# Gate projections of the stick-breaking heads moved into a filler queue, with an earlier start of the fillers

## The chip, the cores and the metric

The kernel runs on one core of a Trainium2 chip. The metric is the device time of one execution in microseconds (us), lower is better. A core has a matrix engine (TensorE, called PE in the profile, with its weight loads as PEld), VectorE (DVE), ScalarE (ACT), GpSimd (POOL) and a queue engine for transfers (SyncE, SP). Transfers are started from the queues of SP, ACT and POOL.

## The reference

Two layers of a decoder trunk, on 1024 rows of width 1024 in f32. Each layer normalises its input with a modulation computed from a conditioning vector, makes one wide projection of it, runs two attentions in parallel and merges them:

```python
mod = jax.nn.silu(c) @ ada_w + ada_b
shift, scale, gate = jnp.split(mod, 3, axis=-1)
h = rms_norm(x, norm_g) * (1 + scale[:, None]) + shift[:, None]
proj = h @ w_in
(sb_q, sb_k, sb_v, sb_z, n_q, k_c, v_c, k_s, v_s, k_w, v_w, n_z, n_g, m_a, m_b) = jnp.split(...)
a = stick_breaking_attention(heads(sb_q, 8), heads(sb_k, 8), heads(sb_v, 8))
a = a.reshape(B, S, 512) * jax.nn.silu(sb_z)
...
b = native_sparse_attention(q, kc, vc, ks, vs, kw, vw, n_g)   # softmax, 8 heads
b = b * jax.nn.silu(n_z)
y = jax.nn.sigmoid(m_a) * (a @ w_proj_a) + jax.nn.sigmoid(m_b) * (b @ w_proj_b)
return x + gate[:, None] * (y @ w_out)
```

Stick-breaking attention uses sigmoids of the scores and a running product in place of a softmax. `sb_z` is the gate projection that the change moves; `n_z` is the sparse heads' gate. Each is 512 columns wide.

## The kernel before

A projection is computed in f32 precision from three products of split operands (high x high, high x low, low x high), so a unit of 128 x 512 outputs takes 24 matmuls (`mm3_gen`, L188 to L199). A group is 256 columns of the weights: four units of 128 columns by 512 rows, or eight units of 128 rows by 256 columns for values. Units are accumulated in the PSUM tile "proj", which has two buffers, and then evicted by ScalarE and VectorE. Weights are loaded from SP, split by ScalarE and VectorE, and loaded one group ahead in the order of a list (`plan_layer`, `take`).

A layer has these stages.

1. `early` (L703): keys and values of the sparse heads, the compressed keys and values, a loop of eight value units (`n_unit`, L808 to L811), the query groups, and then four groups of gate projections (L819 to L838): first the two of the sparse heads, then the two of the stick-breaking heads. A gate unit is evicted by a Sigmoid on ScalarE (L830) and a product on VectorE (L831) and stored in DRAM (`SZ`). Beside the gate units run the modulation steps: one loads 512 KB of `ada_w` (tile "ada", two buffers) from SP, and VectorE adds it, scaled, to an accumulator (L362, L364). Layer 0 has 24 steps (its own gate and the next layer's scale and shift), layer 1 has 8. Two are written behind each unit, from the first gate unit on. `issue_after` keeps a step's VectorE instruction behind that unit's product; the load on SP is free of it. When all groups are done, `gate_rows` and `cols` turn the accumulators into rows and columns with small matmuls on PE (L411, L373).
2. `nsa`: sparse attention, as a list of jobs: 8 compressed-score jobs and 32 head jobs (2 groups x 4 query blocks m x 4 heads). Its scores go through Exp on ScalarE (L1006, L1097, L1099).
3. `sb`: stick-breaking attention, 8 heads x 4 query blocks m. Its scores go through Sigmoid (L1245, L1246), VectorE's scan (L1249) and product (L1250).
4. `output`: merging and the output projection.

Beside stages 2 and 3 run the fillers: generators of projection matmuls in the queue `fill`. `queue_projections` puts in two query, two key and two value groups of the stick-breaking heads (kind "sb") and then eight groups of the merging gates (kind "gate", evicted by a plain copy, L1271). `run_jobs` writes the bursts of a job's value products together with the scores of the next job, and after each burst calls `pump`, which writes filler matmuls for a share of the job's planned time. The planned costs are 0.213 us for a 512-column matmul and 0.107 us for a 256-column one; the planned times of the jobs are `nsa_us` and `sb_us` by m, `cmp_us` for a compressed-score job, and `start_us` for the first scores of a stage. `drain_fill("sb")` between the stages writes what is left of the "sb" groups, `drain_fill()` after stage 3 all that is left.

What is written last is not always what runs last: the framework orders the instructions of each engine again, by the written order as priority and by its own estimate of when inputs are ready. Every engine then works through its order strictly, each instruction waiting for its inputs. The build puts an ACT_TABLE_LOAD on ScalarE ahead of an activation whose function is not in the table loaded last.

## Time and profile before

| what | us |
|---|---|
| median of 3 runs | 2232.81 |
| lowest and highest run | 2227.79, 2235.55 |
| the profiled execution | 2227.61 |
| its span, first to last instruction | 2225.8 |
| PE busy in the span | 2124.4 |
| VectorE busy | 1573.0 |
| ScalarE busy | 1129.9 |

The profile is one execution. Its times count from the span's start. Matmuls overlap, so PE's busy time holds the tail of each; what counts for PE is how far apart the starts are. In layer 0 the early stage ends at about 291, sparse attention at about 690, stick-breaking attention at about 954; in layer 1 at about 1374, 1778 and 2040. A wait is put down to the instruction that came last by the profile.

### The profile page before, as it was taken

What the parts mean: (1) busy time and instruction counts of PE and PEld (TensorE: products, weight loads), DVE (VectorE), ACT (ScalarE), POOL (GpSimd) and SP (SyncE); (2) the same over time, 40 slices, a digit from 0 to 9 for tenths busy, and PEclk for the clock granted to TensorE, in tenths of its full rate; (3) what the DMA queues carried; (4) which work ended last, traced back from release to release, by engine and by line L of the source; (5) the groups of instructions that cost most, each with busy time, mean ns of one, the idle gap of its engine ahead of it and who ended that gap; (6) DMA issues with size and microseconds to landing.
All of it is one profiled execution on the core that took longest, in us unless ns stands there. A gap on an engine that the chain in (4) does not pass through costs nothing.

```text
span 2225.8 us, 36846 instructions
## 1 busy us (share of the span) xinstructions
PE 2124.4 (95%) x13128; PEld 1833.5 (82%) x13128; DVE 1573.0 (71%) x3722; ACT 1129.9 (51%) x2489; POOL 73.0 (3%) x242
## 2 busy tenths in 40 slices
PE   4999999999999999999999998999999999999999
PEld 3898778988887777779889986889898877777899
DVE  5768558868765877886766852887788487787643
ACT  4433147656565655663433421665666465656410
POOL 2200000000000000010011000000000000001000
PEclk8999999999999999999999999999999999999999
DMA  7545852253116445275555355222522364534443
GB/s 287 113 136 189 251 154 81 91 152 94 64 48 159 128 130 129 81 245 177 164 151 161 107 192 141 90 90 82 146 92 68 97 151 113 146 98 166 148 124 104
DMA packets 254104, 297.05 MB, mean 133 GB/s; under 512 B 38888, under 2 KB 201568, under 8 KB 253920
## 3 DMA queue, kind: packets, MB, share of 16 engines
q1 hardware_dynamic: 213152, 250.65, 37.4%
q10 hardware_dynamic: 36224, 29.37, 5.1%
q0 software_dynamic: 4544, 14.68, 2.3%
q8 instruction: 103, 1.69, 0.3%
q14 instruction: 81, 0.66, 0.1%
HBM read 206.28 MB, written 83.89 MB: 130 GB/s over the span
## 4 chain that ended last, share of the span: by engine, by line
PE 66%; DVE 18%; DMA 7%; issue 4%; ACT 3%; POOL 1%; SPq 0%; ACTq 0%; DVEq 0%; POOLq 0%
PE proj L194 15%; PE proj L198 15%; PE proj L196 15%; PE tr L885 5%; DVE C L1249 4%; PE av L905 4%; PE av L904 3%; PE sc L872 3%; PE sc L873 3%; DVE wl L137 3%; DMA ada<-in_ada_w 2%; DVE E L1250 2%; DVE w L137 2%; DMA q<-QK 1%; DMA actlo<-AD 1%
## 5 line engine op out<-in xcount | busy, mean ns | idle before, releaser
L194 PE MATMUL proj<-acthi,w 128*128 128x512 f32 x1312 | 537.6, 410 | 3.0 <-ACT acthi L136 2.2
L196 PE MATMUL proj<-actlo,w 128*128 128x512 f32 x1312 | 538.0, 410 | 0.0
L198 PE MATMUL proj<-acthi,w 128*128 128x512 f32 x1312 | 537.2, 409 | 0.0
L136 ACT CAST w<-raw 128x512 fp32r<-128x512 f32 (+1 forms) x296 | 183.3, 623 | 227.3 <-PE proj L198 129.7
L194 PEld LDWEIGHTS proj<-acthi,w 128*128 128x128 f32 x1312 | 250.2, 191 | 43.6 <-ACT acthi L136 2.7
L137 DVE TENSOR_TENSOR wl<-tr,wh 128x512 fp32r<-128x512 f32 (+2 forms) x432 | 257.0, 611 | 40.7 <-ACT wh L136 38.3
L196 PEld LDWEIGHTS proj<-actlo,w 128*128 128x128 f32 x1312 | 250.0, 191 | 38.1 <-DVE actlo L137 0.8
L198 PEld LDWEIGHTS proj<-acthi,w 128*128 128x128 f32 x1312 | 249.6, 190 | 37.1 <-DVE w L137 0.2
L137 DVE TENSOR_TENSOR w<-raw,w 128x512 fp32r<-128x512 f32 (+1 forms) x296 | 202.5, 689 | 81.9 <-ACT w L136 80.6
L136 ACT CAST wh<-tr 128x512 fp32r<-128x512 f32 (+2 forms) x432 | 221.3, 527 | 76.4 <-PE tr L885 71.3
L194 PE MATMUL proj<-w,acthi 128*128 128x256 f32 (+1 forms) x768 | 221.5, 289 | 5.4 <-DVE s L137 2.4
L905 PE MATMUL av<-wl,V 128*128 128x256 f32 (+1 forms) x864 | 217.6, 285 | 7.6 <-DVE wl L137 7.4
L198 PE MATMUL proj<-w,actlo 128*128 128x256 f32 (+1 forms) x768 | 221.1, 288 | 0.0
L196 PE MATMUL proj<-w,acthi 128*128 128x256 f32 (+1 forms) x768 | 220.0, 286 | 0.0
L904 PE MATMUL av<-wh,V 128*128 128x256 f32 (+1 forms) x864 | 216.7, 271 | 1.2 <-DVE o L923 0.5
L1249 DVE TENSOR_TENSOR_SCAN C<-C 128x128 f32<-128x128 f32 (+7 forms) x128 | 172.7, 1350 | 55.0 <-ACT C L1245 54.5
L885 PE MATMUL tr<-ident,E 128*128 128x128 f32 x1152 | 187.4, 276 | 24.2 <-DVE E L1250 23.4
L885 PEld LDWEIGHTS tr<-ident,E 128*128 128x128 f32 x1152 | 139.1, 140 | 68.1 <-DVE E L1250 35.4
L905 PEld LDWEIGHTS av<-wl,V 128*128 128x128 f32 x864 | 162.7, 188 | 31.0 <-DVE wl L137 19.7
L872 PE MATMUL sc<-kk,q 128*128 128x512 f32 (+3 forms) x512 | 176.8, 346 | 8.8 <-DVE mx L1085 4.1
L873 PE MATMUL sc<-kk,q 128*128 128x512 f32 (+3 forms) x512 | 175.5, 343 | 0.0
L904 PEld LDWEIGHTS av<-wh,V 128*128 128x128 f32 x864 | 163.0, 189 | 13.7 <-ACT wh L136 3.6
(247 smaller groups left out, 3902.8 us busy)
## 6 DMA issues: line engine op xcount, KB each, us to landing
raw<-in_w_in SPq DMA_DIRECT2D x168, 256.0 KB, 3.0
ada<-in_ada_w SPq DMA_DIRECT2D x48, 512.0 KB, 5.1
kk<-QK SPq DMA_DIRECT2D x48, 512.0 KB, 8.6
q<-QK ACTq DMA_DIRECT2D x64, 256.0 KB, 4.2
QK<-s SPq DMA_DIRECT2D x32, 512.0 KB, 3.0
MD<-sz SPq DMA_DIRECT2D x64, 256.0 KB, 2.5
QK<-s SPq DMA_DIRECT2D x48, 256.0 KB, 3.9
VD<-s SPq DMA_DIRECT2D x48, 256.0 KB, 2.0
```

What stands on the lines that cost most here:

```text
L136: nc.scalar.copy(hi, src)
L137: nc.vector.tensor_tensor(lo, src, hi.bitcast(F32), ALU.subtract)
L194: nc.tensor.matmul(ps, lh, rh, start=(x == 0), stop=False)
L196: nc.tensor.matmul(ps, lh, rl, start=False, stop=False)
L198: nc.tensor.matmul(ps, ll, rh, start=False, stop=(x == n - 1))
L872: nc.tensor.matmul(ps, q, k[:, 0, c0:c1], start=True, stop=False)
L873: nc.tensor.matmul(ps, q, k[:, 1, c0:c1], start=False, stop=not masks)
L885: nc.tensor.transpose(pt[:, x * P:x * P + P], b, self.ident)
L904: nc.tensor.matmul(ps[:, c:d], lhsT, hi[:, a:b], start=(first and x == 0), stop=False, skip_group_check=True)
L905: nc.tensor.matmul(ps[:, c:d], lhsT, lo[:, a:b], start=False, stop=(last and x == n - 1), skip_group_check=True)
L1249: nc.vector.tensor_tensor_scan(rev, rev, rev, 1.0, ALU.mult, ALU.bypass)
L1250: nc.vector.tensor_tensor(e[:, 0:nk], e[:, 0:nk], c[:, 1:nk + 1], ALU.mult)
```

## The change

Four things are changed.

- The two gate groups of the stick-breaking heads leave `early`. They become fillers of kind "sb" at the head of the queue, evicted by a new helper `silu_gate` with the same Sigmoid, product and store as before.
- The modulation steps are written earlier: one behind each of the eight value units, then two behind each of the eight gate units that stay. The tile "ada" has four buffers.
- `run_jobs` first writes fillers for a planned time `start`, ahead of the first scores: 12.0 us for the sparse part, 1.5 us for the stick-breaking part. Another 1.5 us are spread over the first scores, where it was 3.0.
- The planned times of the stick-breaking jobs grow from 1.34, 2.87, 4.77, 6.04 to 1.55, 3.35, 5.4, 6.8 us.

```diff
-        self.sb_us = (1.34, 2.87, 4.77, 6.04)
+        self.sb_us = (1.55, 3.35, 5.4, 6.8)
         self.cmp_us = 1.48
-        self.start_us = 3.0
+        self.start_us = 12.0
...
-    def run_jobs(self, jobs):
+    def run_jobs(self, jobs, start):
+        self.pump(start)
         for n in range(len(jobs) + 1):
...
-            us = jobs[n - 1][2] if n else self.start_us
+            us = jobs[n - 1][2] if n else 1.5
...
-            a = self.tl(pool, [P, D], F32, "ada", bufs=2)
+            a = self.tl(pool, [P, D], F32, "ada", bufs=4)
...
             w = self.take()
+            steps = []
+            self.gate, gate_rows = self.mod_gate(l, pool, steps)
+            if l + 1 < self.depth:
+                cols = self.mod_ab(l + 1, pool, steps)
+
+            def mod_steps(n, ins):
+                with tc.issue_after(ins.ins):
+                    for f in steps[:n]:
+                        f()
+                del steps[:n]
+
             for t in range(NT):
                 ps = self.n_unit(w, t, act, 280)
-                self.store_v(ps, t, 8)
+                ins = self.store_v(ps, t, 8)
                 nc.scalar.activation(self.G[:, t, :], ps[:, 256:280], AF.Sigmoid)
+                mod_steps(1, ins)
...
-            for z in range(4):
+            for z in range(2):
                 w = self.take()
-                if z == 0:
-                    steps = []
-                    self.gate, gate_rows = self.mod_gate(l, pool, steps)
-                    if l + 1 < self.depth:
-                        cols = self.mod_ab(l + 1, pool, steps)
                 for u in range(2):
                     for half in range(2):
-                        ps = self.t_unit(w, u, half, act)
-                        s = self.tl(self.stage, [P, 512], F32, "sz")
-                        nc.scalar.activation(s, ps, AF.Sigmoid)
-                        ins = nc.vector.tensor_tensor(s, ps, s, ALU.mult)
-                        with tc.issue_after(ins.ins):
-                            for f in steps[:2]:
-                                f()
-                        del steps[:2]
-                        r0 = z * 256 + u * 128
-                        nc.sync.dma_start(self.SZ[r0:r0 + P, half * 512:half * 512 + 512], s)
+                        mod_steps(2, self.silu_gate(self.t_unit(w, u, half, act), z * 256 + u * P, half))
...
+    def silu_gate(self, ps, r0, half):
+        nc = self.nc
+        s = self.tl(self.stage, [P, 512], F32, "sz")
+        nc.scalar.activation(s, ps, AF.Sigmoid)
+        ins = nc.vector.tensor_tensor(s, ps, s, ALU.mult)
+        nc.sync.dma_start(self.SZ[r0:r0 + P, half * 512:half * 512 + 512], s)
+        return ins
...
-            self.run_jobs(jobs)                     # nsa
+            self.run_jobs(jobs, self.start_us)
...
-            self.run_jobs(jobs)                     # sb
+            self.run_jobs(jobs, 1.5)
...
-                    if what == "qk":
+                    if what == "z":
+                        self.silu_gate(ps, r0 + u * P, half)
+                    elif what == "qk":
...
+        for z in range(2):
+            self.fill.append(("sb", t_group("z", 512 + z * 256)))
         for a in range(2):
             self.fill += [("sb", t_group("qk", 512 + a * 256)), ("sb", t_group("qk", a * 256)), ("sb", v_group(a * 4))]
```

`split` and `store_v` now return their VectorE instruction, so that `issue_after` can name it.

## Rows read from the trace of the kernel before

**Rows 1.** Page, part 1: busy us, share of the span, instructions.

```profile
PE 2124.4 (95%) x13128; PEld 1833.5 (82%) x13128; DVE 1573.0 (71%) x3722; ACT 1129.9 (51%) x2489; POOL 73.0 (3%) x242
```

**Rows 2.** PE in order of time, layer 1's first scores: start, us, what.

```profile
1373.60 0.67 PE L194 MATMUL proj<-acthi,w 128*128 128x512 f32 x1
...
1380.84 0.39 PE L194 MATMUL proj<-acthi,w 128*128 128x512 f32 x1
...
1382.24 0.40 PE L194 MATMUL proj<-acthi,w 128*128 128x512 f32 x1
1389.16 1.86 PE L996 MATMUL sc<-KCS,q 128*128 128x16 f32 x8 [6.52 <-DMA q<-QK]
...
1393.14 0.63 PE L198 MATMUL proj<-acthi,w 128*128 128x512 f32 x1
1393.57 0.63 PE L194 MATMUL proj<-acthi,w 128*128 128x512 f32 x1
```

**Rows 3.** Busy us (instructions) per stretch: PE, PEld, DVE, ACT, POOL, PEclk, DMA, GB/s.

```profile
100.00:130.00 30.00, 26.66 (x201) 25.30 (x200) 14.83 (x50) 9.20 (x25) 0.00 (x0) 1.00 0.66 201
194.00:239.00 45.00, 45.00 (x200) 36.43 (x200) 30.41 (x54) 10.80 (x20) 0.00 (x0) 1.00 0.80 250
310.00:370.00 60.00, 59.10 (x368) 49.56 (x368) 54.20 (x206) 45.96 (x130) 0.32 (x2) 1.00 0.27 84
700.00:730.00 30.00, 26.60 (x159) 20.22 (x158) 27.87 (x38) 21.84 (x50) 0.89 (x9) 1.00 0.51 133
730.00:950.00 220.00, 207.63 (x1185) 167.41 (x1183) 175.92 (x234) 134.10 (x297) 9.21 (x57) 1.00 0.43 120
1388.00:1392.00 4.00, 2.84 (x12) 2.68 (x12) 0.76 (x4) 0.23 (x1) 0.00 (x0) 0.50 1.03 204
1810.00:2035.00 225.00, 211.96 (x1211) 170.80 (x1209) 180.18 (x241) 137.48 (x304) 7.13 (x54) 1.00 0.44 120
```

**Rows 4.** 730 to 950: PE's waits (us, times, longest), then the chain's shares.

```profile
PE tr L885 <- DVE E L1250: 9.3, 15, 1.0
PE av L905 <- DVE wl L137: 3.0, 8, 0.7
...
by line: DVE C L1249 17.7%; DVE E L1250 10.0%; PE proj L196 9.7%; PE proj L198 9.5%; PE proj L194 9.3%; PE tr L885 8.4%; DVE wl L137 5.3%; PE av L905 5.1%; issue 5.0%; PE av L904 4.0%; PE sc L873 2.5%; PE sc L872 2.4%; DVE w L137 2.0%; ACT 
```

**Rows 5.** PE in order of time, layer 0's first sparse scores.

```profile
303.81 1.04 PE L996 MATMUL sc<-KCS,q 128*128 128x16 f32 x8 [0.17 <-DMA q<-QK]
```

**Rows 6.** PE in order of time, end of layer 1's stick-breaking part.

```profile
2021.65 0.55 PE L885 MATMUL tr<-ident,E 128*128 128x128 f32 x3 [0.91 <-DVE E L1250]
...
2031.50 0.55 PE L885 MATMUL tr<-ident,E 128*128 128x128 f32 x3 [0.84 <-DVE E L1250]
...
2051.29 0.79 PE L194 MATMUL proj<-acthi,w 128*128 128x512 f32 x1 [2.23 <-ACT acthi L136]
```

**Rows 7.** ACT in order of time, layer 1: ACTq issues transfers.

```profile
1372.69 8.19 ACTq L942 DMA_DIRECT2D q<-QK  x4
```

**Rows 8.** 194 to 285 by line: busy us, mean ns, idle us before.

```profile
L364 DVE SCALAR_TENSOR_TENSOR acc<-ada,silu_c,acc 128x1024 f32<-128x1024 f32 x21 | 27.0, 1284 | 20.3 <-DMA ada<-in_ada_w 20.3
...
L830 ACT ACTIVATE sz<-proj 128x512 f32<-128x512 f32 x15 | 9.0, 599 | 43.5 <-PE proj L198 39.6 <-DVE sz L831 3.9
```

**Rows 9.** ACT in order of time, the first instructions.

```profile
0.74 1.28 ACT L514 ACT_TABLE_LOAD   x1 [0.74 <-PEq L1452]
2.03 0.20 ACT L514 ACTIVATE warm<-ones 128x1 f32<-128x1 f32 x1
```

**Rows 10.** Lines L1006 and L1245: table loads, ns, first and last start.

```profile
L1006 ACT ACT_TABLE_LOAD  x2: 1283/1283/1283, 297.6 to 1380.9; - x2
...
L1245 ACT ACT_TABLE_LOAD  x2: 1283/1283/1283, 692.7 to 1778.7; - x2
```

**Rows 11.** Page, part 6: transfers, count, KB each, us to landing.

```profile
ada<-in_ada_w SPq DMA_DIRECT2D x48, 512.0 KB, 5.1
```

More of the change, by code (lines that the diff above doesn't have):

```diff
@@ L136, in split @@
         nc.scalar.copy(hi, src)
-        nc.vector.tensor_tensor(lo, src, hi.bitcast(F32), ALU.subtract)
+        return nc.vector.tensor_tensor(lo, src, hi.bitcast(F32), ALU.subtract)
     def rsqrt(self, pool, ss, n, inv, tag, on_pool=False):
@@ L848, in store_v @@
         src = ps[:, 0:256].rearrange("p (h d) -> p h d", d=HD)
-        self.split(src, vt[:, :, 0:64], vt[:, :, 64:128])
+        ins = self.split(src, vt[:, :, 0:64], vt[:, :, 64:128])
         nc.sync.dma_start(self.VD[t * P:(t + 1) * P, h0:h0 + 4, :], vt.bitcast(F32))
+        return ins
     def load_stack_k(self, pool, row, tag="kk"):
```

## The prediction

> **What bounds the kernel now.** I read the page's busy times first [rows 1]: the matmul engine (PE) is busy for 95% of the span, VectorE for 71%, ScalarE for 51%. A busy PE is not PE at its peak: in a dense stretch two neighbouring 512-column projections begin 0.23 us apart while each is shown as 0.39 us long [rows 2]. So a gap shown as idle hides about 0.16 us more. The change keeps the number of matmuls; it can win nothing but waits, and lose nothing but new ones.
>
> The table by stretches [rows 3] says where waits are. The first half of the gate projections in layer 0 (194 to 239) has none: PE is busy for 45.00 of 45 us, ScalarE for 10.80. In the first jobs of sparse attention (310 to 370) PE is busy for 59.10 of 60, but VectorE for 54.20 and ScalarE for 45.96: three engines are close to full. In stick-breaking attention PE is idle for 3.4 of the first 30 us (700 to 730), then for 12.4 of 220 and, in layer 1, 13.0 of 225. Who ends those waits [rows 4]: VectorE's product after the scan (9.3 us, 15 waits) and its low parts (3.0 us, 8). The chain in that stretch lies on VectorE for 17.7 + 10.0 + 5.3 + 2.0 = 35%.
>
> Single waits remain. In layer 1 PE has nothing but fillers after 1373.60, begins the last at 1382.24 and then waits 6.52 us until the queries of the first sparse job land at 1389.16 [rows 2]; the granted clock behind that idle time is 0.50, the lower level (1.2 of 2.4 GHz), and matmuls start 0.43 us apart for a while [rows 2, 3]. In layer 0 the same place costs 0.17 us [rows 5]: there the fillers ahead of the scores lasted long enough. At the end of layer 1's stick-breaking part PE waits 0.91 and 0.84 us in the last job, then 2.23 us for an activation half [rows 6].
>
> **The change, part by part.** The planner counts 0.213 us per 512-column matmul, 20.45 us per group of 4 units, 20.54 us per value group. The profile's spacing is 0.233 us (the seven starts from 1380.84 to 1382.24 give 1.40 / 6), so a planned us is 1.09 us of PE. Before, a layer queues 122.9 us of "sb" and 163.6 us of "gate" filler, 286.5; the sparse part asks for 3.0 + 8 x 1.48 + 8 x 19.03 = 167.1, so 119.4 is left for the stick-breaking part, which asks for 3.0 + 8 x 15.02 = 123.2: the queue runs dry about 3.8 planned us before its end. After, two gate groups (8 units, 40.9 planned, 8 x 24 x 0.233 = 44.7 us of PE) join: 327.4. The sparse part asks for 12.0 + 1.5 + 164.1 = 177.6, stick-breaking for 1.5 + 1.5 + 8 x 17.1 = 139.8, and 10.0 is left to drain. So the 44.7 us that leave the dense early stage come back in three places: 11.5 us before the first sparse scores, 22.3 us spread over the stick-breaking jobs, 10.9 us at the end. Each is worth the waits that it covers.
>
> *Front of the sparse part.* 56 matmuls (13.1 us) now stand ahead of the first scores. In layer 1 it is 15.6 us from 1373.6 to 1389.2, of which 9.0 were covered; the new cover leaves about 2.5 us. That is worth 4.0 us of wait and the slow matmuls (about 13 at 0.43 instead of 0.23, 2.6 us): 6.5 us, bounds 2 and 9.3. The lower bound is there since ScalarE spends 8.19 us on issuing the query loads [rows 7] and evicts nothing meanwhile; with two PSUM buffers the third unit can be held up. Layer 0: 0, bounds -2 and +2.
>
> *Stick-breaking jobs.* 22.3 us more filler a layer against 12.4 + 23 x 0.16 = 16 us of waits and some 5 in the first 30 us, 21 in all. What falls into time that VectorE paces is free; by the chain that is 35%, 7.8 us a layer, 15.6 in all. Bounds: 0 (the fillers land where PE sets the pace) and 21 a layer.
>
> *End.* A queue that isn't dry covers the last job's waits, 0.91 + 0.84 a layer and their hidden parts (layer 0 repeats the pattern), and in layer 1 the 2.23 us: 6 us in all, bounds 2 and 8.
>
> *Activation tables.* This is the price. A gate unit ends in a Sigmoid (599 ns, [rows 8]); the sparse jobs run on Exp. The trace has 5 table loads: one at the start, one at the first Exp and one at the first stick-breaking Sigmoid of each layer, each 1283 ns [rows 9, 10]. So the two functions don't share a table. Of a layer's 8 queued Sigmoids two finish inside the 12 us ahead of the scores, before any Exp; the other six come one by one, 5.1 planned us apart, among jobs of 1.97 and 4.16 planned us with four Exps each. Each costs a load to Sigmoid and one back: 12 loads, 15.4 us of ScalarE a layer, in the stretch of 60 us that holds 45.96 us of it already: 61.4 of 60. Queued behind them are the high parts of transposed tiles, for which VectorE's low parts and then PE's value products wait. But a load stands ahead of the instruction that needs it and can run while that one's input is awaited, and the 14.0 us of ScalarE's idle time there are such waits. I take half on the path, 7.7 us a layer, 15.4 in all; bounds 0 and 30.8.
>
> *Modulation loads.* 24 loads of 512 KB in layer 0 (8 in layer 1, [rows 11]) and as many accumulations of 1284 ns [rows 8] move from the first twelve of sixteen gate units to the eight value units and all eight gate units that stay. In 100 to 130 VectorE is busy for 14.83 of 30 us, so 8 x 1.28 = 10.3 us fit, but PE already loses 3.3 us there and DMA stands at 0.66 [rows 3]. In the gate stage 21 accumulations waited 20.3 us for their loads [rows 8] beside a PE that never stopped; four buffers send a pair of loads one unit earlier. Now the last pair is due with the last gate unit, and the columns of the next layer's modulation wait for it, where four units stood behind. On SP a load that waits for its buffer holds up value stores and the weights of the query groups. I take 2 us for the value units (both layers) and 2 us for the end of layer 0's early stage; bounds -1 and 10.
>
> *The rest.* A gate eviction uses VectorE for one product where a query or key eviction uses it for one subtraction; some 6 such units a layer take the place of plain copies in the sparse part: 1 us in all, bounds 0 and 4. The gate rows are read back in stick-breaking jobs only, long after.
>
> Sum: -6.5 - 15.6 - 6 + 15.4 + 4 + 1 = -7.7 us. On the profiled execution (2227.61, its span 2225.8) that is 2219.9. That execution lies 5.2 us under the median of the three; I carry the difference to the median: 2232.8 - 7.7 = **2225.1**.
>
> **The rivals.**
> 1. *The table loads hide* in ScalarE's waits, and the price drops from 15.4 to about 1: -22 us, 2211. For it: the idle time is nearly as large as the loads. Against: VectorE, which waits for ScalarE's high parts, is at 90% there.
> 2. *ScalarE becomes the bound of the first sparse jobs* (slower). It decides from the point where the loads exceed what idle ScalarE time can take, and 61.4 us in 60 is past it. Then all 30.8 us are on the path, and with half of the stick-breaking gain the sum is -6.5 - 7.8 - 6 + 30.8 + 5 = +15.5, 2248. For it: all five loads of the trace came on an idle engine, so what a load costs right behind other work isn't in the 1283 ns. Against: behind a load nothing comes; the warm-up's ends at 2.03 and the next activation begins at 2.03 [rows 9]. The Trainium skill (ScalarE: Activation LUTs, What ACT_TABLE_LOAD costs) counts a drain of about 1380 ns beside the 1283, 2.66 us a switch; by it, as an estimate, a layer's 12 switches would want 32 us of ScalarE, 18 us more than the stretch has idle, and the sum would be about +13 us. No load of this trace follows work closely enough to show that drain.
> 3. *The change doesn't do what it says.* The order on PE is not the program's (fillers ran ahead of the scores in both layers before, too), so the 12 us may replace only what was moved up anyway, and the extra fillers of the stick-breaking jobs may land on time that PE paces: gains and prices cancel, about 0, 2233.
>
> **How the numbers follow.** A measurement of this kernel can tell about 0.3%, 6.7 us, from no change. Forecast 0.42 (-20 to -2, a bit over half of it beyond 6.7), rival 1 0.22, rival 2 0.22, rival 3 0.14. Faster: 0.25 + 0.22 = 0.47; same: 0.17 + 0.14 = 0.31; slower 0.22. The range reaches from rival 1 with half of the stick-breaking gain's upper room (about -29, 2204) to rival 2 (2247). The forecast's own range is 2213 to 2231.
>
> **What would show it.** 29 table loads instead of 5, the 24 new ones between the first sparse scores and some 70 us later; idle PE there up by 8 us a layer if I am right, by 1 in rival 1, by 15 in rival 2. The wait before layer 1's first sparse scores under 2.5 us, with the clock at its upper level. Idle PE in each stick-breaking part down from 16 to 8 us. No wait of 2 us at layer 1's end. The gate stage shorter by 44.7 us in each layer. I would be wrong if the early stage shrank by clearly less than that, or if the queued gate units stood elsewhere than ahead of the first scores.

## The result, and the profile after

| what | before | after |
|---|---|---|
| median, us (after: 4 runs beside runs of before) | 2232.53 | 2245.51 |
| lowest to highest of after, us | | 2241.76 to 2246.65 |
| ratio of the medians, 95% interval | | 1.0059 [1.0040, 1.0078] |
| the profiled execution, us | 2227.61 | 2245.80 |
| its span, us | 2225.8 | 2244.0 |

The change costs 13 us. The two profiled executions lie 18.2 us apart, since that of before lies some 5 us under its median.

Page of after, part 1, which answers [rows 1], and the engine line of its part 4:

```profile
PE 2134.3 (95%) x13128; PEld 1840.7 (82%) x13128; DVE 1577.4 (70%) x3722; ACT 1160.6 (52%) x2513; POOL 72.3 (3%) x242
...
PE 66%; DVE 15%; DMA 7%; ACT 5%; issue 5%; POOL 1%; SPq 0%; ACTq 0%; DVEq 0%; POOLq 0%
```

PE runs the same 13128 matmuls. ScalarE has 24 instructions and 30.7 us more. No engine's total explains a loss of 18 us.

The busy times hide a part of PE's waits, so I made a tally of the trace: for each form of matmul the median spacing of two neighbouring starts in before; what the spacings have above it in sum counts as stall. All kernels here come to 2032 us of spacing without stall; the rest is in this table (us of stall per stage, profiled executions; the columns are explained with the experiments):

| stage | before | after | after again | e5 | e4 | e11 | e10 | e16 |
|---|---|---|---|---|---|---|---|---|
| early, layer 0 | 43.8 | 49.4 | 48.4 | 48.7 | 50.0 | 49.2 | 48.3 | 49.8 |
| to the first sparse scores | 5.1 | 7.3 | 5.6 | 5.1 | 5.7 | 7.2 | 5.7 | 4.1 |
| sparse, to the first stick-breaking scores | 22.5 | 30.1 | 29.5 | 24.2 | 26.0 | 24.4 | 21.5 | 21.5 |
| stick-breaking | 32.6 | 28.0 | 28.4 | 32.4 | 24.5 | 25.5 | 21.3 | 21.4 |
| output of layer 0, early of layer 1 | 9.6 | 23.2 | 24.5 | 15.8 | 20.5 | 17.1 | 16.4 | 12.0 |
| layer 1: to the first sparse scores | 8.2 | 2.4 | 3.0 | 7.7 | 8.6 | 1.5 | 2.9 | 3.8 |
| layer 1: sparse | 23.0 | 25.6 | 26.3 | 22.3 | 27.1 | 25.3 | 22.6 | 21.4 |
| layer 1: stick-breaking | 31.2 | 27.6 | 27.3 | 30.7 | 24.6 | 24.2 | 21.3 | 21.3 |
| layer 1: output | 4.1 | 4.3 | 4.2 | 3.5 | 4.1 | 2.6 | 2.0 | 2.4 |
| sum | 180.2 | 197.7 | 197.3 | 190.5 | 191.1 | 177.1 | 162.1 | 157.6 |

Each column is one execution, and single executions scatter. Up to 660 us after, after again (e9), e10 and e13 run the same instructions in the same order on every engine, and yet PE's matmul number 3901 starts 657.7, 655.0, 651.7 and 654.4 us behind its first. So a difference of some 3 us in one row, up to 6 in a sum of rows, can be chance; the medians below decide on the kernels.

The gain at layer 1's first sparse scores is there (5.2 to 5.8 us), and so is a part of that in the stick-breaking jobs (3.6 to 4.6 us a layer). New are 4.6 to 5.6 us in layer 0's early stage, some 7 us up to the first stick-breaking scores of layer 0 and 3 in layer 1, and 14 to 15 us between the end of layer 0's stick-breaking part and the end of layer 1's early stage.

**Front of the sparse part.** PE in after, layer 1 (start, us, what, idle before and its releaser), which answers [rows 2]; 6.52 us of wait have become 0.68:

```profile
1368.05 0.58 PE L1005 MATMUL sc<-KCS,q 128*128 128x16 f32 x4 [0.68 <-DMA q<-QK]
```

A window over it shows the granted clock at 1.00, the upper level (columns as in [rows 3]):

```profile
1366.00:1370.00 4.00, 3.32 (x19) 2.54 (x18) 1.58 (x6) 1.45 (x2) 0.00 (x0) 1.00 1.10 240
```

**Stick-breaking jobs.** Windows of the same lengths in after, without each part's first 30 us, which answer [rows 3]:

```profile
711.00:931.00 220.00, 211.50 (x1193) 171.59 (x1192) 169.91 (x227) 131.67 (x289) 5.01 (x51) 1.00 0.42 115
1798.00:2023.00 225.00, 216.17 (x1217) 175.22 (x1215) 171.13 (x229) 132.62 (x291) 5.01 (x51) 1.00 0.42 114
```

PE's idle time fell from 12.4 to 8.5 and from 13.0 to 8.8 us. But at the head of this part PE now waits for the queries (PE in after, the last filler and the first scores in layer 0, the first scores in layer 1):

```profile
671.09 0.40 PE L196 MATMUL proj<-actlo,w 128*128 128x512 f32 x1
676.19 0.45 PE L881 MATMUL sc<-kk,q 128*128 128x128 f32 x1 [4.70 <-DMA q<-QK]
...
1768.12 0.30 PE L881 MATMUL sc<-kk,q 128*128 128x128 f32 x1 [3.43 <-DMA q<-QK]
```

Before has one such wait, in layer 0, and none in layer 1:

```profile
694.73 0.30 PE L872 MATMUL sc<-kk,q 128*128 128x128 f32 x1 [2.26 <-DMA kk<-QK]
```

**Value units of layer 1.** ScalarE, VectorE, SP and PE of after, in four extracts:

```profile
1222.42 0.59 ACT L136 CAST s<-tr 128x512 fp32r<-128x512 f32 x1 [1.43 <-DMA VD<-s]
1228.74 0.37 ACT L136 CAST s<-proj 128x256 fp32r<-128x256 f32 x1 [5.72 <-DMA QK<-s]
1229.60 0.19 ACT L823 ACTIVATE G<-proj 128x24 f32<-128x24 f32 x1 [0.49 <-DVE s L137]
...
1229.14 0.42 DVE L137 TENSOR_TENSOR s<-proj,s 128x256 fp32r<-128x256 f32 x1 [5.41 <-ACT s L136]
...
1220.32 0.33 SPq L858 DMA_DIRECT2D VD<-s  x1
1221.52 0.33 SPq L361 DMA_DIRECT2D ada<-in_ada_w  x1
1222.12 3.94 SPq L776 DMA_DIRECT2D QK<-s  x4
...
1225.56 0.27 PE L198 MATMUL av<-xs,w 128*128 128x192 f32 x1
1229.84 0.40 PE L194 MATMUL proj<-w,acthi 128*128 128x280 f32 x1 [4.01 <-ACT G L823]
...
1231.20 0.44 PE L196 MATMUL proj<-w,acthi 128*128 128x280 f32 x1
1231.44 0.44 PE L198 MATMUL proj<-w,actlo 128*128 128x280 f32 x1
```

Read it from below. PE stands for 4 us, since both PSUM buffers wait for evictions. The eviction on ScalarE waits 5.72 us, not for PE but for a store out of the staging tile "s" (QK<-s): the tile has two buffers, and neither is free until its keys or values have left it. On SP a modulation load (L361, 512 KB) stands between those stores. Behind the wait matmuls of 280 columns start 0.23 us apart, not 0.13; the granted clock there is 0.56:

```profile
1230.00:1233.50 3.50, 3.50 (x17) 3.50 (x18) 2.29 (x3) 0.56 (x2) 0.00 (x0) 0.56 0.68 164
```

The accumulations themselves no longer wait for their loads (by line, which answers [rows 8]):

```profile
L365 DVE SCALAR_TENSOR_TENSOR acc<-ada,silu_c,acc 128x1024 f32<-128x1024 f32 x28 | 35.8, 1277 | 0.1
```

**End of layer 0's stick-breaking part.** POOL, ScalarE and PE of after:

```profile
958.96 2.06 POOL L1352 DMA_DIRECT2D actlo<-AD  x3 [13.83 <-PE proj L198]
964.54 2.05 POOL L1352 DMA_DIRECT2D actlo<-AD  x3 [3.52 <-PE proj L198]
...
965.58 1.14 ACT L136 CAST acthi<-actlo 128x512 fp32r<-128x512 f32 x2 [1.84 <-DMA actlo<-AD]
...
966.25 0.50 PE L194 MATMUL proj<-acthi,w 128*128 128x512 f32 x1 [1.78 <-ACT acthi L136]
```

The output stage loads the attention's result into the activation halves that the fillers read. POOL issues the loads into a half only when the last filler matmul on that half is done ("<-PE proj L198"). In after the last filler is evicted 15.0 us behind the last merge of attention, in before 3.0 us ahead of it; the loads start 7.4 to 14.4 us behind that merge, in before from 14.4 us ahead of it (POOL of before):

```profile
939.93 2.10 POOL L1339 DMA_DIRECT2D actlo<-AD  x3 [5.87 <-PE proj L196]
```

From the last job's last matmul on the strict mask (936.7) up to the first matmul on the merged tile (yh, 1014.9) there are 7.1 us of stall, in before 2.8. In layer 1 the wait that the remainder was to cover is still there (2.23 us in [rows 6]):

```profile
2057.59 0.50 PE L194 MATMUL proj<-acthi,w 128*128 128x512 f32 x1 [1.74 <-ACT acthi L136]
```

**The clock behind the waits.** In nine stretches of after, the one at 1230 among them, the granted clock is at its lower level; before has five. In a tally of the same kind 24.0 and 16.9 us of the stall lie inside these stretches, so some 7 of the 17 us between the two come with the lower clock (after again has 22.2 us there, e11 15.5, e10 13.9, e16 9.0). Three that before has no match for, behind a wait for sparse keys at 461.8 and two waits in layer 0's output stage:

```profile
462.50:465.70 3.20, 3.20 (x17) 3.20 (x16) 1.51 (x6) 1.95 (x6) 0.00 (x0) 0.50 0.19 75
967.70:970.90 3.20, 3.20 (x9) 2.48 (x8) 3.14 (x6) 3.14 (x7) 0.00 (x0) 0.50 1.04 368
1022.30:1025.50 3.20, 3.20 (x14) 3.03 (x15) 2.45 (x8) 0.75 (x2) 0.54 (x1) 0.50 0.45 157
```

**Table loads.** ScalarE of after, by line (count, busy us, mean ns, idle us before):

```profile
L847 ACT ACT_TABLE_LOAD x12 | 15.4, 1283 | 0.2
L1106 ACT ACT_TABLE_LOAD x8 | 10.3, 1283 | 0.1
L1015 ACT ACT_TABLE_LOAD x4 | 5.1, 1283 | 0.1
L1108 ACT ACT_TABLE_LOAD x2 | 2.6, 1283 | 0.0
L1254 ACT ACT_TABLE_LOAD x2 | 2.6, 1283 | 1.4 <-issue 1.4
L515 ACT ACT_TABLE_LOAD x1 | 1.3, 1283 | 0.7 <-PEq L1465 0.7
```

They are 29, as worked out. What they cost the kernel is a matter for the experiments.

### The profile page after: what moved, and what is told of

Its sections match the earlier page's. It is cut to its first block, busy times and chain, and to the rows that moved or that the text cites. A ratio compares the mean times of both kernels' runs of the same rounds, so it can differ in the third digit from the quotient of the medians.

```text
span 2244.0 us, 36874 instructions
## 1 busy us (share of the span) xinstructions
PE 2134.3 (95%) x13128; PEld 1840.7 (82%) x13128; DVE 1577.4 (70%) x3722; ACT 1160.6 (52%) x2513; POOL 72.3 (3%) x242
## 4 chain that ended last, share of the span: by engine, by line
PE 66%; DVE 15%; DMA 7%; ACT 5%; issue 5%; POOL 1%; SPq 0%; ACTq 0%; DVEq 0%; POOLq 0%
PE proj L198 15%; PE proj L194 15%; PE proj L196 15%; PE tr L894 6%; DVE C L1258 4%; PE av L914 3%; PE sc L881 3%; PE av L913 3%; PE sc L882 3%; DVE E L1259 2%; DVE w L137 1%; DVE wl L137 1%; DMA q<-QK 1%; DMA kk<-QK 1%; DMA actlo<-AD 1%
## 5 line engine op out<-in xcount | busy, mean ns | idle before, releaser
L198 PE MATMUL proj<-acthi,w 128*128 128x512 f32 x1312 | 538.9, 411 | 0.0
L198 PEld LDWEIGHTS proj<-acthi,w 128*128 128x128 f32 x1312 | 249.9, 190 | 35.8
L198 PE MATMUL proj<-w,actlo 128*128 128x256 f32 (+1 forms) x768 | 222.9, 290 | 0.0
L894 PE MATMUL tr<-ident,E 128*128 128x128 f32 x1152 | 188.2, 275 | 21.5 <-DVE E L1259 19.7
L881 PE MATMUL sc<-kk,q 128*128 128x512 f32 (+3 forms) x512 | 178.1, 348 | 13.9 <-DMA q<-QK 8.1
L914 PEld LDWEIGHTS av<-wl,V 128*128 128x128 f32 x864 | 162.8, 188 | 27.9 <-DVE wl L137 15.8
```

Of the source, the lines that this page charges most:

```text
L198: nc.tensor.matmul(ps, ll, rh, start=False, stop=(x == n - 1))
L881: nc.tensor.matmul(ps, q, k[:, 0, c0:c1], start=True, stop=False)
L894: nc.tensor.transpose(pt[:, x * P:x * P + P], b, self.ident)
L914: nc.tensor.matmul(ps[:, c:d], lhsT, lo[:, a:b], start=False, stop=(last and x == n - 1), skip_group_check=True)
```

## The experiments

The theory after the traces: the loss is made by the modulation loads beside the value units, by the remainder of the queue that is drained behind the last job, and by the short front of the stick-breaking part. Its rivals are the 24 table loads (rival 2) and that the moved work only changes places (rival 3). The four groups of runs had medians of before of 2228.1, 2228.8, 2229.0 and 2229.5 us; ratios go by these. "Left" is what the planner still has in the queue behind the last job, in planned us; "dry" says that it has nothing from so many planned us ahead of the end. Stall of a kernel that has no column above is from the same tally.

**Tables: e1_tanh.** After, but a queued gate unit computes the same value by Tanh, which needs no load between the Exps:

```diff
-        nc.scalar.activation(s, ps, AF.Sigmoid)
-        ins = nc.vector.tensor_tensor(s, ps, s, ALU.mult)
+        nc.scalar.activation(s, ps, AF.Tanh, scale=0.5)
+        ins = nc.vector.scalar_tensor_tensor(s, s, 1.0, ps, ALU.add, ALU.mult)
```

(the missing factor 0.5 goes into the product where the gate is used)

> The changed kernel, with the queued gate units' Sigmoid computed as (1 + tanh(x/2))/2: Tanh on ScalarE, one sum-and-product on VectorE, the factor 1/2 where the gate is read back. Same number of instructions on each engine. If Tanh is served by the table that serves Exp, the table loads fall from 29 to 5. Theory A (three causes: table loads in the sparse part, modulation loads beside the value units, the queue's remainder holding up the output stage's loads): the stall of PE in the sparse parts falls by 7.6 + 2.6 = 10 us, the rest stays; 2235, about the time of before. Theory B (the table loads alone made it slower; rival 2 of the prediction): it falls by 20 us or more, to 2225 or less, faster than before. Theory C (the loads hide): no change, 2245.

2240.43 us, 1.0051 [1.0036, 1.0066]. The trace has 5 loads again. Windows over the first sparse jobs, after and then e1, layer 0:

```profile
270.00:360.00 90.00, 87.99 (x527) 73.39 (x525) 72.52 (x261) 76.64 (x175) 0.32 (x2) 1.00 0.24 72
```
```profile
270.00:360.00 90.00, 88.39 (x534) 75.03 (x533) 74.18 (x263) 62.34 (x164) 0.32 (x2) 1.00 0.25 76
```

ScalarE is freed of 14.3 us in 90; PE's idle time falls by 0.4 us only, and PE starts 7 matmuls more. The kernel gains about 1 us of its 13 (12.3 over before, the changed kernel again 13.3, e9 below). The theory of the table loads falls.

**Modulation steps back: e2_mods_late.** After, with the steps beside the gate units again, three behind each in layer 0 and one in layer 1:

```diff
-                mod_steps(1, ins)
...
-                        mod_steps(2, self.silu_gate(...))
+                        mod_steps(per, self.silu_gate(...))   # per = 3 or 1
```

> The changed kernel with the modulation steps put back beside the gate units that stay: three behind each of the eight in layer 0, one in layer 1, none beside the value units; four buffers kept. Theory A (the modulation loads delay the stores of keys and values, so that the two staging buffers, then ScalarE, then PE wait): the 4.0 us wait of PE in layer 1's value units goes, and the early stages lose 5 to 6 us of stall in each layer, unless layer 0's gate stage now ends with a wait for its loads (up to 8 us more there, since 24 loads have 45 us); layer 1 alone: -7 us. Total 2234 to 2241. Theory B (table loads alone): no change in layer 1's early stage, 2245.

2245.23, 1.0078 [1.0064, 1.0093]: no gain. Layer 0's early stage lost 3.7 us of stall against after, but the wait ahead of the first sparse scores rose by 4.2 us: three steps behind each gate unit end too late. In layer 1 half of the wait at the value units stayed (1.90 of 4.01 us), since four buffers let SP take four of the loads ahead of the value units; only the VectorE step is held back. A poor test, which led to e5 and e8.

**The early steps alone: e5_before_mods.** Before, with the modulation steps and four buffers as in after, nothing else:

```diff
-            a = self.tl(pool, [P, D], F32, "ada", bufs=2)
+            a = self.tl(pool, [P, D], F32, "ada", bufs=4)
...
+                with tc.issue_after(ins.ins):     # behind each value unit
+                    for f in steps[:1]:
+                        f()
+                del steps[:1]
```

> The kernel before with one part of the change alone: the modulation steps behind the eight value units and then two behind each of the first eight gate units, four buffers; all four gate groups stay in the early stage, fillers and planned times as before. Theory A (the modulation loads disturb the value units: their transfers delay the stores on which the two staging buffers wait): the stall of PE in the early stages rises by 4 to 6 us in layer 0 and by 5 to 7 us in layer 1 (a wait of 2 to 4 us at its value units), time +8 to +12 us. Theory B (the waits at the value units come from what the changed queue does elsewhere): same within 3 us.

2239.9, 1.0047 [1.0035, 1.0059]: this part alone costs 11 us, 10 by the tally. By the table, 4.9 of them are in layer 0's early stage and 6.2 between the layers, there 5.2 in layer 1's value units. The first of three products in the value units' matmuls, which waits for evictions, by form, before and then e5 (busy, mean ns, idle before and its releasers):

```profile
L194 PE MATMUL proj<-w,acthi 128*128 128x280 f32 x128 | 38.1, 297 | 2.9 <-ACT G L811 2.1 <-ACT rpx L643 0.8
```
```profile
L194 PE MATMUL proj<-w,acthi 128*128 128x280 f32 x128 | 38.7, 302 | 5.7 <-ACT G L815 5.7
```

**The old front: e4_start3.** After, with nothing ahead of the first scores and 3.0 planned us spread over them, in both parts; some 20 left:

```diff
-            us = jobs[n - 1][2] if n else 1.5
+            us = jobs[n - 1][2] if n else 3.0
...
-            self.run_jobs(jobs, self.start_us)
+            self.run_jobs(jobs, 0.0)
...
-            self.run_jobs(jobs, 1.5)
+            self.run_jobs(jobs, 0.0)
```

> The changed kernel with the start as it was: no fillers written ahead of the first scores, 3.0 planned us spread over them; the rest as changed (10.5 us more are then left for the end of each layer). The step of the prediction holds if the wait before layer 1's first sparse scores comes back (about 6.5 us and matmuls at the lower clock for some us) and the time rises by 5 to 10 us. If the order of the engines puts fillers ahead of the scores by itself, the wait stays away and the time is the same within 3 us.

2240.96, 1.0057 [1.0044, 1.007]. The wait ahead of layer 1's sparse scores is back, 5.6 us of it, so that step of the prediction is right in its place. Yet the total didn't move: the first stick-breaking scores wait 1.27 and 0.67 us here, where after again has 4.23 and 3.60, and the stick-breaking parts have 3.9 and 2.7 us less stall. PE in e4, then in after again, layer 0:

```profile
660.51 0.30 PE L881 MATMUL sc<-kk,q 128*128 128x128 f32 x1 [1.27 <-DMA kk<-QK]
```
```profile
672.74 0.45 PE L881 MATMUL sc<-kk,q 128*128 128x128 f32 x1 [4.23 <-DMA q<-QK]
```

**A longer front and a dry queue: e3_tanh_start26, e11_start26.** e1 and after, each with 26 planned us ahead of the first sparse scores; dry by about 4:

```diff
-        self.start_us = 12.0
+        self.start_us = 26.0
```

> As e1_tanh, and 26 instead of 12 planned us of fillers ahead of the first sparse scores, so that the queue runs dry about 4 planned us before the end of the stick-breaking part, as it did before the change, with the same filler rate in all jobs. Theory A (the remainder of the queue reads the activations whose buffers the output stage's loads reuse, so they start late): the transfers of the output stage's activations start 8 to 10 us earlier against the last job, the output front of layer 0 loses 4 to 6 us of stall and the 2 us wait of layer 1's end goes: 6 to 9 us under e1_tanh. Theory B (a remainder at the end only covers waits): 0 to 3 us over e1_tanh.

> The changed kernel with 26 instead of 12 planned us at the front of the sparse part, the Sigmoid kept: as e3_tanh_start26, but with the table loads that are left (three Sigmoids a layer among the Exps instead of six, so some 12 extra loads in all instead of 24). If the loads cost little, -4 to -1 against before like e3 (-3.8); if each costs its 1.28 us, 15 us more than e3, +11.

2224.45, 0.9983 [0.9972, 0.9994] and 2226.19, 0.9987 [0.9975, 0.9999]. With the job rates of after, 14 planned us moved from the remainder to the front of the sparse part are worth 16 us, where I had expected 6 to 9; 7.4 of them lie between the layers. e11 has 17 table loads, since half of the queued gate units now finish ahead of the scores, and e3 has 5: these 12 make no difference beyond the scatter.

**Dry by denser jobs: e6_tanh_dry. A longer front with a remainder: e7_tanh_front26_rest.**

```diff
 # e6: e1 with
-        self.sb_us = (1.55, 3.35, 5.4, 6.8)
+        self.sb_us = (1.72, 3.72, 6.0, 7.55)
 # e7: e3 with
+        self.sb_us = (1.39, 3.0, 4.85, 6.11)
```

> As e1_tanh (12 us of fillers at the front, +12 us against before), with the planned times of the stick-breaking jobs raised to 1.72, 3.72, 6.0, 7.55, so that the queue is dry about 5 planned us before their end. With e3_tanh_start26 and e7_tanh_front26_rest this tells the longer front from the dry end. If the dry end made e3 faster than e1 by 15 us (the remainder of the queue reads the activations' buffers and holds up the output stage's loads), this run gains 10 us or more over e1: +2 or less. If the longer front did it, this run stays at +9 to +13.

> As e3_tanh_start26 (26 us of fillers at the front, -4 us against before), with the planned times of the stick-breaking jobs lowered to 1.39, 3.0, 4.85, 6.11, so that some 10 planned us are left for the end, as in the changed kernel. If the dry end made e3 faster than e1, this run loses 8 us or more against e3: +4 or more. If the longer front did it, it stays at -4 to 0.

e6: 2229.31, 0.9997 [0.9987, 1.0007], 12 us better than e1. e7: 2233.56, 1.002 [1.001, 1.0031], some 8 us worse than e3. Dry kernels win both times. But here the job rate moves with the remainder: e7's stick-breaking parts have 28.7 and 28.5 us of stall, e3's 24.5 and 24.3. These pairs don't tell the two apart. e3 and e11 against e1 and after keep the rate, but there the front grows by what the remainder loses; no run here changes the remainder alone.

**Layer 1's steps late: e8_tanh26_l1late, e15_l1late.** e3 and after, with layer 1's eight steps made beside its gate units, where the tile has two buffers, so that SP can't take the loads early:

```diff
-            a = self.tl(pool, [P, D], F32, "ada", bufs=4)
+            a = self.tl(pool, [P, D], F32, "ada", bufs=2 if part == 2 and l else 4)
...
+                if z == 0 and l:          # in the gate groups' loop
+                    self.gate, gate_rows = self.mod_gate(l, pool, steps)
```

> As e3_tanh_start26, and layer 1's eight modulation steps back beside its gate units (one behind each), with two buffers there; layer 0 stays as changed. Theory A: the wait at layer 1's value units (2.4 us and slow matmuls behind it in e3) goes, 4 to 6 us less: -8 to -10 us against before, faster than both kernels. Theory B (that wait is not from the modulation loads): same as e3, -4.

> The changed kernel (+12 us) with layer 1's eight modulation steps back beside its gate units, one behind each, with two buffers in that layer; layer 0 as changed. The wait at layer 1's value units (3.9 us and slow matmuls) goes: +6 to +9. If its transfers only move the wait elsewhere, +11 to +13.

e8: 2222.26, 0.9968 [0.9956, 0.998], 3 us better than e3. e15: 2241.31, 1.0048 [1.0031, 1.0065], 1 to 2 us better than after again, with runs from 2233.5 to 2243.5. The value units' stall falls from 6.7 to 2.8 us in e15, to 1.2 in e8, so the place is right. The totals moved by less than I expected, in e15 (+11.8) by no more than the second case allowed, that the wait only moves. e16 below shows the gain more clearly.

**The changed kernel again: e9_after_again.** No edit.

> The changed kernel itself, on the chip of the next three runs, as their measure: +11 to +15 us against before. With e1_tanh (+12.3) it also bounds the table loads: if they cost nothing that counts, the two agree; by the prediction's 15.4 us on the path this run would be at +27.

2242.33, 1.0054 [1.0035, 1.0072]: 13.3 us over before on this chip.

**The front of the stick-breaking part: e10_sbfront.** After, with one number changed; dry by about 4:

```diff
-            self.run_jobs(jobs, 1.5)
+            self.run_jobs(jobs, 15.3)
```

> The changed kernel with one number changed: 15.3 instead of 1.5 planned us of fillers ahead of the first stick-breaking scores, so that the queue is dry about 4 planned us before that part's end; rates in all jobs and the front of the sparse part as changed, the Sigmoid kept. Theory D (the remainder that is drained behind the last job costs 8 to 13 us, as e1 against e6 and e7 against e3 say): 8 to 13 us under the changed kernel, +0 to +5 against before, and the output stage's activations are loaded before the last job ends. Theory E (e6 gained by its denser fillers in the stick-breaking jobs, e3 by its longer front, neither by the dry end): 3 us or less under the changed kernel, from the waits at the first stick-breaking scores alone.

2212.76, 0.9925 [0.9906, 0.9944]: 29.6 us better than e9, 16.3 better than before, more than twice the 8 to 13 that theory D allowed. The first stick-breaking scores have no wait. The two windows of the stick-breaking jobs in e10:

```profile
700.00:920.00 220.00, 213.12 (x1205) 173.10 (x1204) 166.25 (x226) 128.71 (x281) 5.01 (x51) 1.00 0.45 122
1784.00:2009.00 225.00, 217.28 (x1223) 176.01 (x1222) 173.05 (x230) 134.25 (x294) 5.01 (x51) 1.00 0.42 115
```

Idle PE is 6.9 and 7.7 us, and POOL issues the output stage's first loads at 935.69, 1 us behind the last job's last matmul on the strict mask (934.6), where it is 22 us in after (958.96 against 936.7):

```profile
935.69 2.09 POOL L1352 DMA_DIRECT2D actlo<-AD  x3 [9.19 <-PE proj L196]
939.65 2.14 POOL L1418 DMA_DIRECT2D gt<-MD  x4 [1.88 <-DVE E L1259]
944.38 0.76 POOL L1352 DMA_DIRECT2D actlo<-AD  x1 [2.58 <-PE proj L196]
```

By the table the 35 us between the profiled executions of e9 and e10 are 8.0 up to the first stick-breaking scores, 7.1 and 6.0 in those parts, 8.1 between the layers, 3.7 in layer 1's sparse part and 2.2 at the end. Of the first 8.0 only the 4.23 us of the wait are the edit's: 3.3 us are the wait for sparse keys at 459 us and the lower clock behind it, which e9 has and e10 has not in instructions that are the same in both.

**Front, but a remainder: e13_sbfront_rest.** e10 with thinner jobs, about 10 left:

```diff
-        self.sb_us = (1.55, 3.35, 5.4, 6.8)
+        self.sb_us = (1.39, 3.0, 4.85, 6.11)
```

> As e10_sbfront (-16 us against before), with the planned times of the stick-breaking jobs lowered to 1.39, 3.0, 4.85, 6.11, so that about 10 planned us are again left for the end. If the dry end is most of e10's gain, this run falls back to +0 to +8; if the cover of the first stick-breaking scores is, it stays at -14 to -8.

2233.42, 1.0018 [1.0007, 1.0029]: 20 us of e10's gain are gone. Of the tally's 24.7 us, 6.9 and 7.3 are in the stick-breaking parts (28.2 and 28.6 of stall) and 6.6 in the two output rows of the table. So the front alone isn't enough. Rate and remainder change together here; the places of the stall, in the thinner jobs and in the output stages, speak for both.

**The front without the gate units: e14_before_sbfront.** Before, with 13.8 planned us ahead of the first stick-breaking scores, paid by thinner jobs:

```diff
-        self.sb_us = (1.34, 2.87, 4.77, 6.04)
+        self.sb_us = (1.19, 2.54, 4.22, 5.35)
...
-            self.run_jobs(jobs)                     # sb
+            self.run_jobs(jobs, 13.8)
```

> The kernel before with 13.8 planned us of its own fillers ahead of the first stick-breaking scores, taken from the jobs' planned times (1.19, 2.54, 4.22, 5.35), so that the queue is dry where it was. If the place of the fillers is what counts and not their number, this gains some of what e10 gained: -12 to -4. If the stick-breaking jobs need their filler rate and the moved gate units are what makes the front affordable, the thinner jobs give it back: -3 to +5.

2245.12, 1.007 [1.0057, 1.0083]: worse than before by 15.6 us, far outside both of my cases. E's products hold PE for longer (before, then e14, by line, busy us, mean ns, idle before; e10 has 12.0 us for this releaser):

```profile
L885 PE MATMUL tr<-ident,E 128*128 128x128 f32 x1152 | 187.4, 276 | 24.2 <-DVE E L1250 23.4 <-DVE wl L137 0.3
```
```profile
L887 PE MATMUL tr<-ident,E 128*128 128x128 f32 x1152 | 190.7, 277 | 37.3 <-DVE E L1252 36.3 <-DVE wl L137 0.5
```

Without the moved gate units there is too little filler for both a front and the jobs; with them, put where e10 puts them, the kernel gains 16 us. So moving them isn't an exchange of places that cancels by itself, as rival 3 has it: where they go decides.

**All together: e12_tanh_sbfront_l1late, e16_sbfront_l1late.** e10 with layer 1's steps late as in e15; e12 with Tanh, e16 with Sigmoid:

```diff
 # both edits, of e10 and of e15 (e12: and of e1)
-            self.run_jobs(jobs, 1.5)
+            self.run_jobs(jobs, 15.3)
...
+            a = self.tl(pool, [P, D], F32, "ada", bufs=2 if part == 2 and l else 4)
```

> The queue's surplus at the front of the stick-breaking part (15.3) instead of at the front of the sparse part (26), with Tanh and layer 1's modulation steps beside its gate units as in e8_tanh26_l1late (-6.5 against before). If what counts is that the queue is dry at the end and some dense work covers the first scores, this is at -9 to -4: the longer front of the sparse part is not needed. If the longer front matters by itself, -3 to +2.

> e12_tanh_sbfront_l1late (-22 us against before) with the Sigmoid, that is e10_sbfront with layer 1's modulation steps late. If the table loads cost 1 us or so, -22 to -19, faster than e10 by 3 to 6. If the loads count once the other waits are gone, -18 or more.

2207.25, 0.9902 [0.9882, 0.9921] and 2207.13, 0.9899 [0.9887, 0.9912]: 22 us faster than before, the best kernels here. The late steps are worth 6 us beside e10. In e16 the staging tile's eviction, with no load between the stores, waits 1.94 us where it waits 5.72 in after:

```profile
1200.79 0.37 ACT L136 CAST s<-proj 128x256 fp32r<-128x256 f32 x1 [1.94 <-DMA QK<-s]
```

The two have 5 and 29 table loads and the same time.

## Why the prediction was wrong, point by point

It said 2225.1 and faster; the kernel is 13 us slower than before. Three of its steps failed on the slow side: the modulation loads were put at +4 and cost 10 to 11, the remainder at the end was put at -6 and gains nothing, and the shorter front of the stick-breaking part had no term and costs 5.6. The gain of the stick-breaking jobs was put at twice its size. The table loads, put at +15.4 and worth 0 to 1, hid a part of this by luck: with 1 in their place the same sum says 2211, 35 us off. By its own terms:

- **Front of the sparse part, -6.5: right in place and size.** 5.2 to 5.8 us of stall went, the remaining wait is 0.68 us (under 2.5 was named), the clock is at its upper level, and e4 brought the stall back. Layer 0 was put at 0 within 2; it came out at +0.5 to +2.2.
- **Stick-breaking jobs, -15.6: half of it.** 8.1 to 8.2 us of stall went, both layers taken together. That VectorE paces 35% of the chain was a share of the stretch with before's fillers; it said nothing on where the new ones land. e4, e11 and e10 have the same job rates as after and 24.5, 25.5 and 21.3 us of stall in layer 0's part, after 28.0: where the jobs stand against the queue matters beside the rate. Why it does isn't settled.
- **The step that was left out: the front of the stick-breaking part.** The diff turns 3.0 planned us spread over the first scores into 1.5 ahead of them and 1.5 spread. The change part listed it and gave it no term. It is the same pattern as [rows 2], 6.52 us of wait for queries, that the prediction had just priced for the sparse part: 4.23 us instead of 2.26 in layer 0, 3.60 instead of none in layer 1 (e9). With e4's start they are 1.27 and 0.67, with e10's none.
- **End, -6: no gain came, and the output stage lost time.** The 10.0 planned us that stay in the queue were taken for a cover of the last job's waits. What I didn't follow is who waits for the drained work: the output stage's loads go into the halves that these fillers read. The remainder delays them (958.96 above). 14 planned us moved from it to the front were worth 16 us (e11 against e9; 7.4 between the layers and the rest in other rows of the table, some by a mechanism that I don't have). From the last job's last value product to layer 1's first transposes, which is the output stage, a tally of the same kind has 10.5 us in after and 9.9 in e9, but 3.2 in before, 4.9 in e10 and 5.5 in e11. Yet e3 and e8, dry at the same rate, have 8.6 and 9.0 there. So the late loads are shown, and how much of the stall is their doing is not. The waits of 0.8 to 1.0 us in layer 1's last job and 1.74 behind it stayed.
- **Activation tables, +15.4: oversized.** The count of 29 held exactly. But e1 against e9 and e12 against e16 put the price of 24 loads at 1 and -1 us, and e3 against e11 that of 12 at 1, which is within the scatter. PE's idle time in the first 70 us of the sparse jobs rose from 0.9 and 1.1 us to 1.7 and 1.8: by the 1 us a layer that was named for rival 1, not by 8. The half "on the path" was a guess between 0 and 30.8; rival 1 had it at 1 and was right on that. Rival 2's time, 2248 by its sum (the range has 2247), came out nearly, by causes that aren't its own.
- **Modulation loads, +4: undersized.** e5 measures 10 to 11 us, at or just over the upper bound of 10. The prediction looked at VectorE's time and at the DMA share of 0.66; what fails in layer 1 is the staging tile "s", whose stores share SP and the DMA engines with the loads (5.72 against 1.94 us of wait, after and e16). How layer 0's 4.9 us in e5 come about isn't told apart. The prediction named SP's value stores as held up, and gave them no price. The accumulations' wait for their loads, 20.3 us in [rows 8], is 0.1 in after and bought nothing, since PE never waited for it, as the prediction itself said.
- **The rest, +1:** not told apart from the others.
- **Gate stage shorter by 44.7 us:** layer 0's modulation rows begin at 246.7 instead of 285.3, 38.6 us earlier; the other 6 are about the early stage's new stall (5.6).

Summed, as measured: front -5.2, stick-breaking jobs -8.1, first stick-breaking scores +5.6, modulation loads +11, tables 0 to 1. That is +3 to +4 of the 17 us between the profiled executions of e9 and before. The other 13 us lie between the layers (8.7 of the 14.9 there, which e5 doesn't have) and in layer 0's sparse part (5.0 of the 7.0). Of the 5.0, some 3 are the wait for sparse keys at 459, which is scatter (e10 above). The rest is mostly gone in e11 and e10, which run dry ahead of the end. How much of it is late loads and how much is other placement stays open: e4, with 20 planned us left, has less stall between the layers (20.5) than after again with 10 (24.5).

No rival had these causes: all of them kept the end as a gain or at 0, none had the front of the stick-breaking part, and none had the modulation loads above 5.

## What to carry to other kernels

When work goes into a filler queue, follow its total to the last consumer: what is left behind the last job reads buffers that the next stage wants to load. The fastest kernels here are dry a little ahead of the end and have the surplus in front of a stage's first dependent instruction. A transfer that is moved has to be priced by the stores and staging buffers it then stands beside, too, and not by its own wait alone. A table load on an engine that often waits for its inputs may cost nothing: change the function, as e1 does, before giving it a price.

## What was unexpected of the hardware

A table load right behind other work and right ahead of it cost its 1.28 us and no more. ScalarE of after, layer 1:

```profile
1388.22 0.36 ACT L931 COPY mt<-av 64x256 f32<-64x256 f32 x1 [0.60 <-PE av L914]
1388.61 1.28 ACT L847 ACT_TABLE_LOAD   x1
1389.90 0.60 ACT L847 ACTIVATE sz<-proj 128x512 f32<-128x512 f32 x1
1390.39 0.58 ACT L136 CAST ch<-tr 128x512 fp32r<-128x512 f32 x1
1390.99 1.28 ACT L1108 ACT_TABLE_LOAD   x1
1392.29 0.51 ACT L1108 ACTIVATE ew<-ew,mx 128x256 f32<-128x256 f32 x1
```

The copy ends at 1388.58, the load begins at 1388.61, the activation 1.29 us after that; the load back follows its predecessor by 0.02 us. The Trainium skill (ScalarE: Activation LUTs, What ACT_TABLE_LOAD costs) adds a drain of about 1380 ns to each switch; these rows have no place for it, and the measurement decides.

And one number of the plan, 1.5 or 15.3 us ahead of the stick-breaking scores, moves this kernel by 29.6 us, about twice the 15.0 us of matmuls (13.8 x 1.09) that it puts elsewhere.
